# The in-projection's units in another order: those with the rotary embedding alternate with those without, and the background's share follows the kind

## The chip, the cores and the metric

One Trainium2 chip, one core of it. The metric is the device time of one launch in microseconds; of several runs the median is taken. Five engines work side by side, each with its own queue in order: TensorE (PE in the profile; its weight loads are PEld), VectorE (DVE), ScalarE (ACT), GpSimd (POOL) and SyncE (SP), whose queue starts the transfers. An instruction waits at the head of its queue until what it needs is there, and everything behind it waits too.

## What the kernel computes

One block of a network over 2,048 tokens of width 1,024, with 256 context tokens, all in 32-bit floats:

```python
h  = modulate(layer_norm(x), sh1, sc1);  hc = the same of ctx
q, k, v, u, g = split(h @ w_in)          # 512 columns each; the same of hc
q, k = apply_rope(q), apply_rope(k)      # t1*cos - t2*sin, t2*cos + t1*sin: not on v, u, g
o  = head_norm(softmax(q1 k1) v - lam * softmax(q2 k2) v)   # over tokens and context
u  = centred_conv(u, 4 taps)
r, i = sigmoid(u @ w_gates + b)          # in both directions
a  = exp(-8 r softplus(-lambda));  b = sqrt(1 - a*a) * i * u
y  = (scan(a, b) forwards + scan(a, b) backwards) * gelu(g)
x  = layer_norm(alpha * x + g1 * ([o, y] @ w_out))
x  = layer_norm(alpha * x + g2 * swiglu(modulate(x)))
```

The case is about `h @ w_in` for q, k, v and g, the rotary embedding on q and k, and the recurrence (conv, gates, scans), which runs in the background beside it.

## The kernel before

Every product is made of three matmuls (`mm3`, L142 to L144): both operands are split into a high and a low part, and high·high, high·low and low·high are summed in PSUM. Tokens come in four blocks of 512 (0 to 3) and the context. The stage of this case lies between about 208 and 704 us: the in-projection of blocks 2 and 3 (the first half, `X`), then of blocks 0 and 1 (the second half, `Y`). The normed input of a half lies in SBUF, and `run_units` walks through a list of units. A unit is a kind and a column chunk: `g`, `k` or `q` with c = 0 to 3 (128 columns each), or `v` with c = 0 or 1 (256 columns in two weight tiles).

For each unit `prep_w` loads the weights, casts the high part on ACT (L173) and subtracts it for the low part on DVE (L174, 128x1024). There are two weight tiles, and the next unit's are asked for when a unit begins. The third matmul of a product (L144; for v the second, L143) is the first that reads the low part. Per block of 512 tokens a unit of kind g, k or q is 24 matmuls of 512 columns into one PSUM tile `ps_p`, of which there are four, shared with `ps_v`:

- `g`: ACT copies the tile (L197), SP stores it. The tile is free.
- `k`, `q`: ACT copies (L197), DVE shuffles the copy (L203), multiplies the PSUM tile by cos (L204, which frees it), the shuffled one by sin (L205), and adds (L206); ACT casts the high part (L209), POOL makes the low one (L210). This is the rotary embedding.
- `v`: ACT casts out of PSUM (L248), DVE subtracts (L249).

The recurrence is a generator, `chain`, over four channel blocks: conv (ACT L540, DVE L542), gates (`ps_g`, in PSUM tiles of their own; ACT L571 sigmoids, POOL L573), then the chain proper (ACT L599, L601, L606, L610, in turn with DVE L603, L612, L614, and the four scans L620 and L621 forwards, L623 and L624 backwards; L621 and L624 span 2,048 tokens), POOL L629, and the outputs (L641 to L646 for blocks 2 and 3; L663 to L669 for blocks 0 and 1, only after all g are stored). ACT needs an ACT_TABLE_LOAD where it goes from one of these functions to another. After every block of a unit (for v every 256 tokens) `between` calls `pump(n)`, which issues the next pieces of the chain until their costs, given with each `yield`, sum to n. All of it costs about 280 of these units. A scheduler then puts each engine's instructions in an order; neither list nor pump is the last word, so the order of the built program is shown below.

In the first half the units stand as g0 to g3, v0, v1, k0 to k3, q0 to q3 (q2 and q3 by block), 5.5 after each call. The second half begins with g0 to g3 alone, 5.5 each, then `g_done`, then k0 v0 q0 k1 q1 k2 v1 q2 k3 q3 with 5 a call; call 14 (`over_lru`) issues what is left of the chain, and the ten calls after it two score steps of the attention each (`early`, up to 24).

Of the kernel before, what the change touches and what calls it, by code (L numbers as in the profile page):

```python
# [60 lines left out]
def kernel(ctx: ExitStack, tc: tile.TileContext, x, cx, prm_d, wa1, wa2, b_ada, w_in, w_v, lqk,  # L61
# [7 lines left out]
    def dma(o, i):  # L69
        return nc.sync.dma_start(out=as32(o), in_=as32(i)).ins  # L70
# [82 lines left out]
    with ExitStack() as s12:  # L153
# [61 lines left out]
        def proj_v(p, bl, ws, between, ahead):  # L215

            vw = [w.rearrange("p a k d -> p a (k d)").rearrange("p a (k d) -> p a k d", d=256) for w in ws]
            for b in bl:
                t0, W = blocks[b]
                ht = hts[b]  # L220
                pss = [psum("proj", "ps_v") for _ in range(W // 256)]

                def mms(n, t, half):
                    o = pss[n][:, t * 256:(t + 1) * 256]
                    for k in range(4):
                        h = ht[:, :, 4 * half + k, (2 * n + t) * P:(2 * n + t + 1) * P]
                        w = vw[half][:, :, k]

                        mm3(o, h[:, 0], h[:, 1], w[:, 0], w[:, 1], half == k == t == 0, half == t == 1 and k == 3)

                if b != bl[-1]:
                    for n in range(W // 256):
                        for half in range(2):
                            for t in range(2):
                                mms(n, t, half)
                else:
                    for half in range(2):
                        for n in range(W // 256):
                            for t in range(2):
                                mms(n, t, half)  # L240
                        if half == 0:
                            ahead()
                for n, ps in enumerate(pss):
                    hi = rp.tile([P, 512], F32R, tag="hi", name="vh", bufs=2)
                    lo = rp.tile([P, 512], F32R, tag="lo", name="vl", bufs=2)
                    hm = lambda a: a.rearrange("p (h t d) -> p h t d", h=2, t=2)
                    tm = ps.rearrange("p (t h d) -> p h t d", h=2, t=2)
                    last["act"] = S.copy(hm(hi), tm).ins  # L248
                    last["dve"] = V.tensor_tensor(hm(lo), tm, hm(hi.bitcast(F32)), ALU.subtract).ins  # L249
                    kt = t0 // P + 2 * n  # L250
                    for part, t in ((0, hi), (1, lo)):
                        dma(v_d[p][part, :, :, kt:kt + 2, :], hm(t))
                    between()

        base = {"q": 0, "k": 4, "g": 12}

        def run_units(units, between=lambda: None):

            ws, order_ = {}, []
            for k, c, _ in units:  # L260
                for key in ([(k, c, 0), (k, c, 1)] if k == "v" else [(k, c)]):
                    if key not in order_:
                        order_.append(key)

            def want(i):
                if i < len(order_) and order_[i] not in ws:
                    k, c, *half = order_[i]
                    ws[order_[i]] = prep_w(w_v[c, half[0]] if half else w_in[base[k] + c])

            want(0)  # L270
            for k, c, bl in units:
                if k == "v":
                    i = order_.index((k, c, 0))
                    want(i + 1)
                    proj_v(c, bl, [ws[k, c, 0], ws[k, c, 1]], between, lambda: want(i + 2))
                    continue
                want(order_.index((k, c)) + 1)
                for b in bl:
                    proj(k, c, b, ws[k, c])
                    between()  # L280

        with ExitStack() as s1:
            xp = s1.enter_context(tc.tile_pool(name="xp", bufs=8, reuse_waits="tile"))
# [188 lines left out]
            def ada_pump(n):  # L472
                for _ in range(n):
                    next(ada, None)
# [4 lines left out]
            for n, b in enumerate(order[1:], 1):  # L479
                if n + 1 < len(order):  # L480
                    load_x(order[n + 1])
                hts[b] = new_ht()
                lift(b, xt, range(KD))
                if n + 1 < len(order):
                    xt = norm(order[n + 1])
                for c in range(4):
                    ps = psum("proj", "ps_u")
                    mm_u(b, c, ps, range(KD))
                    put_u(b, c, ps)
                    ada_pump(0 if n == 1 else 2)  # L490
                if b == "c":
                    run_units([("k", c, [b]) for c in range(4)] + [("v", p, [b]) for p in range(2)], lambda: ada_pump(2))
            ada_pump(100)


# [209 lines left out]
        state = {"hold": False, "g_done": False, "end": False, "due": 0.0}  # L705
# [3 lines left out]
        def pump(n):  # L709

            state["due"] += n
            paces.append((last["act"], last["dve"]))
            act, dve = paces[max(0, len(paces) - 1 - 1)]
            while state["due"] > 0:
                if state["end"] or (state["hold"] and not state["g_done"]):
                    state["due"] = 0
                    return
                try:
                    with tc.issue_after(act), tc.issue_after(dve):
                        cost = next(bg)  # L720
                    if cost == "drained":
                        state["hold"] = True
                    else:
                        state["due"] -= cost or 1.0
                except StopIteration:
                    state["end"] = True
# [37 lines left out]

        fold = fold_wo()

        def between_x():
            next(fold, None)
            pump(5.5)

        X, Y = [2, 3], [0, 1]

        with tc.issue_after(last["x"]):
            for b in X:
                load_tabs(b)
        xs = [(k, c) for k in "gvkq" for c in range(2 if k == "v" else 4)]
        run_units([(k, c, X) for k, c in xs[:-2]] + [(k, c, [b]) for b in X for k, c in xs[-2:]], between_x)
        sf.close()
        for b in Y:
            load_ht(b)  # L780
            load_tabs(b)
        run_units([("g", c, Y) for c in range(4)], lambda: pump(5.5))
        state["g_done"] = True

        slots = {}

# [91 lines left out]
        first = s_slots(0, 0)  # L878
        calls = [0]

        def between():
            calls[0] += 1
            if calls[0] < 14:
                pump(5)
            elif calls[0] == 14:
                over_lru()
            else:
                for _ in range(2):
                    early()
# [5 lines left out]
                left[0] -= 1  # L895
                next(first)

        run_units([(k, c if k != "v" else c // 2, Y) for c in range(4) for k in ("kvq" if c % 2 == 0 else "kq")], between)

# [243 lines left out]
    units = [Unit(tb, j) for tb in range(2) for j in range(NJ)]  # L1145
# [25 lines left out]
    with ExitStack() as s4:  # L1171
# [128 lines left out]
        for b in range(NB):  # L1300
            rh = head_norm(b)
            xs = []
# [102 lines left out]
    for n in range(32):  # L1405
        hf, i = n // 16, n % 16
        c = slice(hf * 512, (hf + 1) * 512)
# [106 lines left out]
```

## Time and profile before

| | |
|---|---|
| median of 3 runs | 2916.2 us (2916.05 to 2921.6) |
| the profiled execution | 2915.73 us, span 2913.9 us |
| PE busy over the span | 2765.6 us, 95% |
| DVE busy | 2013.6 us, 69% |
| ACT busy | 1433.6 us, 49% |
| PE, DVE and ACT busy from 387 to 456 us | 51.91, 68.35 and 38.20 of 69 us |
| PE, DVE and ACT busy from 456 to 531 us | 70.14, 51.19 and 60.29 of 75 us |

The first lines are averages over a program that PE bounds nearly everywhere. The last two show that DVE's load is uneven within this stage: full where k and q run beside scans, two thirds where only g runs. What a stage loses is read from PE's waits in it and from the distance of its matmuls. The profile's busy time of PE overlaps from matmul to matmul, so the own time of a stretch is taken below as its matmuls times their distance.

### The profile page before, as it was taken

The page shows a single profiled execution, that of the slowest core. Times are in us where ns is not written, and L with a number is a line of the kernel's source. Part 1 is how long each engine was busy: PE and PEld are TensorE (multiplying, and loading weights), DVE is VectorE, ACT ScalarE, POOL GpSimd, SP SyncE. Part 2 cuts the span into 40 slices and gives each one's busy share as a digit, 9 for nine tenths or more (in the row PEclk, how much of TensorE's full clock was granted, in tenths as well). Part 3 has the DMA queues.
Part 4 walks back from the last instruction along what each step waited for, and adds up shares of the span by engine and source line. Part 5 has one row for each costly group of instructions (what it writes and reads, how often), then busy time and mean ns, then how long its engine had stood idle before and what let it go on. Part 6 is the DMA issues. An engine that isn't in the chain of part 4 may idle for free.

```text
span 2913.9 us, 37631 instructions
## 1 busy us (share of the span) xinstructions
PE 2765.6 (95%) x13452; PEld 2310.3 (79%) x13452; DVE 2013.6 (69%) x3298; ACT 1433.6 (49%) x2039; POOL 1409.1 (48%) x923
## 2 busy tenths in 40 slices
PE   8989879878999999999999899999999999999998
PEld 4868767766899999987777688887888888888886
DVE  7755796586899999995788865558656556335554
ACT  3546668663677777774235533334333334224332
POOL 2004544444788888871354754445544432112443
PEclk9999999989999999999999999999999999999999
DMA  8875637357132222217373433223322237446552
GB/s 328 315 224 177 201 107 274 119 180 224 42 76 76 72 74 61 66 41 278 128 248 101 147 96 87 81 86 115 100 85 80 80 100 258 136 130 188 164 164 90
DMA packets 227804, 407.96 MB, mean 140 GB/s; under 512 B 21400, under 2 KB 110616, under 8 KB 225056
## 3 DMA queue, kind: packets, MB, share of 16 engines
q1 hardware_dynamic: 227616, 405.55, 43.3%
q8 instruction: 106, 1.74, 0.3%
q14 instruction: 82, 0.67, 0.1%
HBM read 281.74 MB, written 123.75 MB: 139 GB/s over the span
## 4 chain that ended last, share of the span: by engine, by line
PE 66%; DVE 7%; ACT 3%; issue 2%; POOL 2%; DMA 2%; SPq 0%; DVEq 0%; ACTq 0%; POOLq 0%
PE ps L143 14%; PE ps L144 14%; PE ps L142 14%; PE ps_s L846 8%; PE pt L927 4%; PE po L921 2%; PE po L922 2%; PE po L920 2%; DVE e L848 1%; PE ps_w L1225 1%; PE ps_w L1226 1%; PE ps_w L1229 1%; PE ps_l L1225 1%; PE ps_l L1229 1%; PE ps_l L1226 1%
## 5 line engine op out<-in xcount | busy, mean ns | idle before, releaser
L848 DVE TENSOR_SCALAR_CACHE_REDUCE e<-ps_s 128x768 f32<-128x768 f32 x384 | 359.6, 951 | 37.0 <-PE ps_s L846 28.5
L864 POOL TENSOR_TENSOR a<-e,e 128x768 f32<-128x768 f32 x192 | 349.3, 1849 | 17.1 <-PE pt L927 12.5
L846 PE MATMUL ps_s<-k,q 128*128 128x384 f32 x1536 | 335.7, 350 | 13.8 <-DVE e L848 12.5
L853 ACT ACTIVATE e<-e,nm 128x2304 f32<-128x2304 f32 x128 | 285.2, 2228 | 50.6 <-DVE nm L852 47.5
L846 PEld LDWEIGHTS ps_s<-k,q 128*128 128x128 f32 x1536 | 267.2, 191 | 29.4 <-DVE e L848 22.4
L1376 ACT CAST hid<-hf 128x512 fp32r<-128x512 f32 x192 | 111.5, 586 | 281.2 <-PE ps L144 266.5
L1377 POOL TENSOR_TENSOR hid<-hf,hid 128x512 fp32r<-128x512 f32 x64 | 83.6, 1306 | 315.9 <-ACT hid L1376 315.9
L931 ACT CAST ah<-pt 128x512 fp32r<-128x512 f32 x288 | 166.1, 582 | 130.1 <-PE pt L927 128.9
L932 DVE TENSOR_TENSOR al<-pt,ah 128x512 fp32r<-128x512 f32 x288 | 196.0, 686 | 34.7 <-ACT ah L931 34.5
L1377 DVE TENSOR_TENSOR hid<-hf,hid 128x512 fp32r<-128x512 f32 (+1 forms) x128 | 95.8, 751 | 157.1 <-ACT hid L1376 157.0
L861 POOL TENSOR_SCALAR e<-e,rr,rn 128x2304 f32<-128x2304 f32 x64 | 146.4, 2288 | 90.3 <-DVE nm L852 49.9
L1053 POOL TENSOR_TENSOR s<-w1r 128x512 f32<-128x512 f32 x44 | 59.3, 1348 | 270.3 <-DMA w1r<-in_w 254.2
L142 PE MATMUL ps_p<-ht,w 128*128 128x512 f32 (+1 forms) x416 | 162.0, 390 | 18.2 <-DVE kf L204 11.6
L927 PEld LDWEIGHTS pt<-ident,a 128*128 128x128 f32 x1152 | 144.2, 141 | 42.8 <-POOL a L864 4.3
L927 PE MATMUL pt<-ident,a 128*128 128x128 f32 x1152 | 174.6, 274 | 3.6 <-POOL a L864 3.4
L144 PE MATMUL ps_p<-ht,w 128*128 128x512 f32 (+1 forms) x416 | 161.2, 389 | 7.6 <-DVE w L174 7.6
L143 PE MATMUL ps_p<-ht,w 128*128 128x512 f32 (+1 forms) x416 | 161.3, 388 | 0.0
L210 POOL TENSOR_TENSOR lo<-kf,hi 128x512 fp32r<-128x512 f32 (+1 forms) x36 | 58.7, 1633 | 177.9 <-ACT hi L209 147.1
L1097 POOL TENSOR_TENSOR v<-v,q 128x512 f32<-128x512 f32 x44 | 72.1, 1639 | 145.1 <-DVE u L1096 145.1
L920 PE MATMUL po<-ah,v 128*128 128x512 f32 x288 | 126.1, 438 | 0.6 <-ACT ah L931 0.6
L921 PE MATMUL po<-al,v 128*128 128x512 f32 x288 | 116.3, 404 | 3.8 <-DVE al L932 2.1
L922 PE MATMUL po<-ah,v 128*128 128x512 f32 x288 | 114.1, 396 | 0.0
(3086 smaller groups left out, 8298.5 us busy)
## 6 DMA issues: line engine op xcount, KB each, us to landing
w1r<-in_w SPq DMA_DIRECT2D x88, 512.0 KB, 3.5
hf<-hid_d SPq DMA_DIRECT2D x64, 512.0 KB, 4.1
hid_d<-hid SPq DMA_DIRECT2D x88, 256.0 KB, 2.2
wraw<-in_w_in SPq DMA_DIRECT2D x32, 512.0 KB, 5.1
adaw<-in_wa SPq DMA_DIRECT2D x32, 512.0 KB, 4.9
q<-q_d SPq DMA_DIRECT2D x64, 256.0 KB, 4.9
oy<-oy_d SPq DMA_DIRECT2D x16, 1024.0 KB, 5.8
x<-in_x SPq DMA_DIRECT2D x29, 512.0 KB, 8.7
```

The lines of the kernel that those rows point to most:

```text
L142: PE.matmul(ps, lhsT=lh, rhs=rh, start=start, stop=False)
L143: PE.matmul(ps, lhsT=lh, rhs=rl, start=False, stop=False)
L144: last["pe"] = PE.matmul(ps, lhsT=ll, rhs=rh, start=False, stop=stop).ins
L846: PE.matmul(ps[:, j, :384], lhsT=q[:, m, part, qt * P:(qt + 1) * P], rhs=kst[h, m][:, c0:c0 + 384], start=(part == 0), stop=(part == 1))
L848: V.tensor_scalar(et[:, cc * 768:(cc + 1) * 768].rearrange("p (a b) -> p a b", a=2), ps[:, :, :384], -0.125, None, ALU.mult, ALU.min, accu ...
L853: S.activation(et, et, AF.Exp, bias=nm[:, m:m + 1], scale=-1.0, accum_out=ss[m])
L864: last["a"] = G.tensor_tensor(a, es[0][:, g * 768:(g + 1) * 768], es[1][:, g * 768:(g + 1) * 768], ALU.add).ins
L920: PE.matmul(po, lhsT=vh, rhs=ah, start=(j == 0), stop=False)
L921: PE.matmul(po, lhsT=vh, rhs=al, start=False, stop=False)
L927: PE.transpose(pt[:, qt * P:(qt + 1) * P], ath[h, b, qt, j // 6][:, (j % 6) * P:(j % 6 + 1) * P], ident)
L932: V.tensor_tensor(al, pt, ah.bitcast(F32), ALU.subtract)
L1377: (G if m in (1, 4) else V).tensor_tensor(t[:, 1], raw[:, 4 * r:4 * r + w], t[:, 0].bitcast(F32), ALU.subtract)
```

## The change

Units now alternate in one list for each half. First half: g0 k0 g1 k1 v0 q0 g2 k2 v1 k3 g3 q1, then q2 and q3 by block. Second half: g0 k0 g1 q0 g2 k1 g3 v0 q1 k2 v1 q2 k3 q3, in one call of `run_units`. `between` gets the kind: 6.8 units of the background after a g or v, 4.2 after a k or q (in the first half 16 calls of each, 176 as before). In the second half `over_lru` comes at call 20, `g_done` after the eighth g block, and the twelve calls after call 20 make two score steps each.

```diff
-        def run_units(units, between=lambda: None):
+        def run_units(units, between=lambda kind: None):
...
-                    proj_v(c, bl, [ws[k, c, 0], ws[k, c, 1]], between, lambda: want(i + 2))
+                    proj_v(c, bl, [ws[k, c, 0], ws[k, c, 1]], lambda: between("v"), lambda: want(i + 2))
...
-                    between()
+                    between(k)
...
+        share = {"g": 6.8, "v": 6.8, "k": 4.2, "q": 4.2}
+        def between_x(kind):
             next(fold, None)
-            pump(5.5)
+            pump(share[kind])
...
-        xs = [(k, c) for k in "gvkq" for c in range(2 if k == "v" else 4)]
+        xs = [("g", 0), ("k", 0), ("g", 1), ("k", 1), ("v", 0), ("q", 0), ("g", 2), ("k", 2), ("v", 1), ("k", 3),
+              ("g", 3), ("q", 1), ("q", 2), ("q", 3)]
...
-        run_units([("g", c, Y) for c in range(4)], lambda: pump(5.5))
-        state["g_done"] = True
+        g_units = [0]
...
-        def between():
+        def between(kind):
             calls[0] += 1
-            if calls[0] < 14:
-                pump(5)
-            elif calls[0] == 14:
+            g_units[0] += kind == "g"
+            state["g_done"] = g_units[0] == 8
+            if calls[0] < 20:
+                pump(share[kind])
+            elif calls[0] == 20:
                 over_lru()
...
-        run_units([(k, c if k != "v" else c // 2, Y) for c in range(4) for k in ("kvq" if c % 2 == 0 else "kq")], between)
+        ys = [("g", 0), ("k", 0), ("g", 1), ("q", 0), ("g", 2), ("k", 1), ("g", 3), ("v", 0), ("q", 1), ("k", 2),
+              ("v", 1), ("q", 2), ("k", 3), ("q", 3)]
+        run_units([(k, c, Y) for k, c in ys], between)
```

What this does to the engines' order is shown at three places. First DVE late in the first half, around the long scans of the second channel block (gate_3081 and gate_3083 before). Before, in the middle of the k and q units:

```order
L174 TENSOR_TENSOR w<-wraw,w 128x1024
L614 SCALAR_TENSOR_TENSOR gate_3083<-A_3311,gate_3083 128x1152
L206 TENSOR_TENSOR kf<-kf,sh 128x512
L620 SCALAR_TENSOR_TENSOR gate_3081<-A_3310,gate_3081 128x256
L204 TENSOR_TENSOR kf<-ps_p,ct 128x512
L205 TENSOR_TENSOR sh<-sh,st__1988 128x512
L623 SCALAR_TENSOR_TENSOR gate_3083<-A_3311,gate_3083 128x256
L203 STREAM_SHUFFLE sh<-kf 128x512
L621 SCALAR_TENSOR_TENSOR gate_3081<-A_3310,gate_3081 128x2048
L206 TENSOR_TENSOR kf<-kf,sh 128x512
L624 SCALAR_TENSOR_TENSOR gate_3083<-A_3311,gate_3083 128x2048
L174 TENSOR_TENSOR w<-wraw,w 128x1024
```

And after, where these scans are gate_2969 and gate_2971, from the weights of q1 to behind the long scans:

```order
L174 TENSOR_TENSOR w<-wraw,w 128x1024
L614 SCALAR_TENSOR_TENSOR gate_2971<-A_3225,gate_2971 128x1152 x2
L204 TENSOR_TENSOR kf<-ps_p,ct 128x512
L205 TENSOR_TENSOR sh<-sh,st__1992 128x512
L620 SCALAR_TENSOR_TENSOR gate_2969<-A_3224,gate_2969 128x256
L206 TENSOR_TENSOR kf<-kf,sh 128x512 x2
L623 SCALAR_TENSOR_TENSOR gate_2971<-A_3225,gate_2971 128x256
L621 SCALAR_TENSOR_TENSOR gate_2969<-A_3224,gate_2969 128x2048
L174 TENSOR_TENSOR w<-wraw,w 128x1024
L624 SCALAR_TENSOR_TENSOR gate_2971<-A_3225,gate_2971 128x2048
L203 STREAM_SHUFFLE sh<-kf 128x512
L204 TENSOR_TENSOR kf<-ps_p,ct 128x512
```

Before, the L204 of k3's and q0's blocks stand ahead of, between and behind the scans, and a unit's weights (L174) behind both long ones. After, k3's rotary ends ahead of them, the next unit is g3, which has none, and the weights stand between the two long scans.

Second, DVE at the border of the halves, from the weights of the third unit of the second half (g2 before, g1 after; the first L174 of each piece) to those of the fourth. Before:

```order
L174 TENSOR_TENSOR w<-wraw,w 128x1024
L612 TENSOR_TENSOR gate_3758<-gate_3758,gate_3757 128x1152
L614 SCALAR_TENSOR_TENSOR gate_3758<-A_4010,gate_3758 128x1152
L542 SCALAR_TENSOR_TENSOR uc<-ub,prm,uc 128x2048 x2
L174 TENSOR_TENSOR w<-wraw,w 128x1024
```

After:

```order
L174 TENSOR_TENSOR w<-wraw,w 128x1024
L203 STREAM_SHUFFLE sh<-kf 128x512
L204 TENSOR_TENSOR kf<-ps_p,ct 128x512
L205 TENSOR_TENSOR sh<-sh,st__4112 128x512
L206 TENSOR_TENSOR kf<-kf,sh 128x512
L620 SCALAR_TENSOR_TENSOR gate_3715<-A_4010,gate_3715 128x256
L542 SCALAR_TENSOR_TENSOR uc<-ub,prm,uc 128x2048
L621 SCALAR_TENSOR_TENSOR gate_3715<-A_4010,gate_3715 128x2048
L542 SCALAR_TENSOR_TENSOR uc<-ub,prm,uc 128x2048
L542 SCALAR_TENSOR_TENSOR uc<-ub,prm,uc 128x256
L203 STREAM_SHUFFLE sh<-kf 128x512
L174 TENSOR_TENSOR w<-wraw,w 128x1024
```

Between the two weights stood four instructions of the chain and the conv; now k0's first rotary block and the shuffle of its second, two scans, one of them long, and three of the conv stand there.

Third, ACT late in the second half: the pieces end with the cast of q1's weights (L173), behind the last sigmoid (L571) of the last channel block; the names are that block's gates (gate_44..) and decays (A_). Before:

```order
L599 ACT_TABLE_LOAD
L599 ACTIVATE A_4758<-gate_4401,spm_1976 128x1152
L606 ACTIVATE A_4758<-A_4758,ones 128x1152
L601 ACTIVATE gate_4401<-gate_4401,spm_1975 128x1152
L571 ACT_TABLE_LOAD
L571 ACTIVATE gate_4403<-ps_g,prm 128x256
L599 ACT_TABLE_LOAD
L599 ACTIVATE A_4759<-gate_4403,spm_1976 128x1152
L197 COPY kf<-ps_p 128x512
L173 CAST w<-wraw 128x1024
```

After:

```order
L571 ACT_TABLE_LOAD
L571 ACTIVATE gate_4438<-ps_g,prm 128x256
L606 ACTIVATE A_4669<-A_4669,ones 128x1152
L601 ACTIVATE gate_4436<-gate_4436,spm_1975 128x1152
L641 ACT_TABLE_LOAD
L641 ACTIVATE gg<-gg 128x512
L599 ACT_TABLE_LOAD
L599 ACTIVATE A_4670<-gate_4438,spm_1976 128x1152
L606 ACTIVATE A_4670<-A_4670,ones 128x1152
L173 CAST w<-wraw 128x1024
```

Between the last sigmoid and the cast stood a table load and two others; now two table loads and five others stand there. The table loads of the whole program go from 59 to 63.

## Rows read from the trace of the kernel before

**Rows 1.** Windows: us, busy PE, PEld, DVE, ACT, POOL (xinstructions), PEclk, DMA, GB/s.

```profile
387.00:456.00 69.00, 51.91 (x218) 41.22 (x216) 68.35 (x76) 38.20 (x49) 30.67 (x18) 0.93 0.43 149
456.00:531.00 75.00, 70.14 (x327) 57.76 (x325) 51.19 (x42) 60.29 (x73) 27.99 (x23) 1.00 0.59 224
531.00:670.00 139.00, 117.34 (x630) 101.76 (x631) 89.69 (x85) 87.71 (x106) 64.01 (x38) 0.90 0.50 171
```

**Rows 2.** Waits of PE, 387 to 456 us: total us, times, longest.

```profile
PE ps_p L142 <- DVE kf L204: 11.6, 2, 9.3
PE ps_p L144 <- DVE w L174: 3.3, 2, 2.2
PE ps_p L142 <- ACT hi L209: 2.1, 1, 2.1
```

**Rows 3.** Timeline of PE around that longest wait: start, us, instruction [idle before].

```profile
433.59 0.77 PE L142 MATMUL ps_p<-ht,w 128*128 128x512 f32 x1 [9.34 <-DVE kf L204]
...
435.00 0.63 PE L142 MATMUL ps_p<-ht,w 128*128 128x512 f32 x1
435.43 0.63 PE L143 MATMUL ps_p<-ht,w 128*128 128x512 f32 x1
...
437.37 0.39 PE L142 MATMUL ps_p<-ht,w 128*128 128x512 f32 x1
437.60 0.40 PE L143 MATMUL ps_p<-ht,w 128*128 128x512 f32 x1
```

**Rows 4.** Waits of PE, 270 to 341 us.

```profile
PE ps_v L142 <- ACT w L173: 6.0, 1, 6.0
PE ps_v L143 <- DVE w L174: 1.5, 1, 1.5
```

**Rows 5.** Timeline of ACT: copies of the first, the last X and the last block.

```profile
219.49 0.57 ACT L197 COPY kf<-ps_p 128x512 f32<-128x512 f32 x1
...
455.36 0.58 ACT L197 COPY kf<-ps_p 128x512 f32<-128x512 f32 x1
...
703.96 0.59 ACT L197 COPY kf<-ps_p 128x512 f32<-128x512 f32 x1
```

**Rows 6.** Groups by shape, 208 to 705 us: busy us, mean ns, idle before.

```profile
L174 DVE TENSOR_TENSOR w<-wraw,w 128x1024 fp32r<-128x1024 f32 x30 | 47.4, 1582 | 31.1 <-ACT w L173 31.0
...
L206 DVE TENSOR_TENSOR kf<-kf,sh 128x512 f32<-128x512 f32 x31 | 35.3, 1137 | 0.3
...
L542 DVE SCALAR_TENSOR_TENSOR uc<-ub,prm,uc 128x2048 f32<-128x2048 f32 x12 | 30.0, 2503 | 14.6 <-ACT uc L540 14.6
...
L203 DVE STREAM_SHUFFLE sh<-kf 128x512 f32<-128x512 f32 x32 | 23.7, 741 | 0.0
...
L612 DVE TENSOR_TENSOR gate<-gate,gate 128x1152 f32<-128x1152 f32 x16 | 22.7, 1423 | 11.2 <-ACT gate L610 11.0
...
L204 DVE TENSOR_TENSOR kf<-ps_p,ct 128x512 f32<-128x512 f32 x31 | 21.2, 684 | 1.0
...
L621 DVE TENSOR_TENSOR_SCAN gate<-A,gate 128x2048 f32<-128x2048 f32 x4 | 19.0, 4739 | 0.0
```

**Rows 7.** Waits of PE, 456 to 531 us.

```profile
PE ps_p L142 <- DMA ht<-ht_d: 1.0, 1, 1.0
```

**Rows 8.** Waits of PE, 531 to 670 us.

```profile
PE ps_v L142 <- DVE kf L204: 5.5, 2, 4.3
PE ps_v L143 <- DVE w L174: 4.6, 3, 3.9
PE ps_v L142 <- ACT w L173: 4.5, 2, 4.0
```

**Rows 9.** Timeline of ACT around a table load in the second half.

```profile
558.86 0.58 ACT L248 CAST vh<-ps_v 128x512 fp32r<-128x512 f32 x1
559.46 1.28 ACT L599 ACT_TABLE_LOAD   x1
560.75 1.26 ACT L599 ACTIVATE A<-gate,spm 128x1152 f32<-128x1152 f32 x1
```

More of the change, by code (lines that the diff above doesn't have):

```diff
@@ L491 @@
                 if b == "c":
-                    run_units([("k", c, [b]) for c in range(4)] + [("v", p, [b]) for p in range(2)], lambda: ada_pump(2))
+                    run_units([("k", c, [b]) for c in range(4)] + [("v", p, [b]) for p in range(2)], lambda _: ada_pump(2))
             ada_pump(100)
@@ L765 @@
         fold = fold_wo()
-        def between_x():
+        share = {"g": 6.8, "v": 6.8, "k": 4.2, "q": 4.2}
+        def between_x(kind):
             next(fold, None)
-            pump(5.5)
+            pump(share[kind])
         X, Y = [2, 3], [0, 1]
```

## The prediction, made before the changed kernel had run

> **What bounds the kernel now.** I read the windows first, because the page's averages hide the stage. From 387 to 456 us DVE is busy 68.35 of 69 us while PE is busy 51.91; from 456 to 531 it is the reverse, PE 70.14 and DVE 51.19 of 75 [rows 1]. So the first half of the in-projection ends on DVE, with k's and q's rotary beside the chain's scans, and the border of the halves, with g alone, ends on PE. The waits of PE name it: 11.6 us for the L204 that frees a PSUM tile, 3.3 for weights, 2.1 for L209, 17.0 in all [rows 2]. The longest, 9.34, is followed by matmuls 0.43 us apart, where later ones are 0.23 apart [rows 3]: the granted clock had fallen to its lower level. Ahead of that stretch PE waits 7.5 us for the weights of v [rows 4]. From 531 to 670 three kinds of wait sum to 14.6 [rows 8].
>
> PE's own work in a half is its matmuls by their distance, 0.227 us for 512 columns (the 0.23 of [rows 3], less rounded) and, as an estimate from that, half of it, 0.115, for 256. A half has 24 unit-blocks of 24 matmuls (130.8 us) and 384 narrow ones of v (44.2). With the background's gates, one channel block is 48 wide and 12 narrow ones, 12.3 us. The first half, from the copy of the first block to that of the last, 219.49 to 455.36, is 235.9 us [rows 5] for 130.8 - 5.4 + 44.2 + 24.6 = 194.2 of matmuls: 41.6 lost. The second, to 703.96, is 248.6 for about 205: 44 lost. The sum below is made against the profiled execution's 2915.7 us; the median is 2916.2, half a us more. I call same what is within 0.2%, 5.8 us, which is about what a measurement of this kernel can tell from no change.
>
> **What is changed in amount.** Matmuls, rotary blocks, chain and weights are the same in number. Four table loads more at 1.28 us [rows 9] are 5.1 us of ACT, and count only where ACT is waited for (below). The background's total share in the first half is unchanged, so what moves is which DVE and ACT work falls beside which matmuls. Four score steps more are asked for early, twelve calls of two instead of ten, but by the order of PE as many stand ahead of the last q in both: nothing, since work that came earlier there would only change its place.
>
> **First half, its end.** Between the weights of g3 and those of q3, DVE has in the new order three L174 (1.58), seven of L603, L612 and L614 (1.42 by L612), four each of L203 (0.74), L204 (0.68) and L205 (about 1), three L206 (1.14), two long scans (4.74) and two short ones (about 1, an estimate from L204 and L206): 4.7 + 10.0 + 3.0 + 2.7 + 4.0 + 3.4 + 9.5 + 2.0 = 39.3 us [rows 6]. PE has 130 matmuls there, 29.5 us. PE therefore loses about 9.8, if DVE is in step with it at the start, in four or five pieces of one to three us, too short for a pause like that of [rows 3]. Before, the 69 us of [rows 1] held 218 matmuls, 49.5 us: 19.5 lost. Gain 9.7. It can be nothing (DVE late at g3 by as much) and at most the whole 19.5.
>
> **First half, v.** v's second weights cannot be cast before the unit ahead has left its weight tile. Before, some 5 us of v's matmuls stood ahead of their first use, and PE waited 6.0 + 1.5 [rows 4]. After, the first channel block's gates stand among v0's matmuls, 10 us by the order, and this wait goes. What is late next is a PSUM tile: v0's last L249 stands behind a long scan and eight more instructions of the chain, and I make PE 6 us late there, at g2, and 1 us at a sigmoid. Of 7.5 plus a stretch at the lower clock, 7 remain: gain 3, between -3 and 7.5.
>
> **The border.** PE waited 1.0 us at most there [rows 7]. After, between the weights of g1 and of q0, DVE has one rotary block (3.5 us), the next one's L203 (0.74), two scans (1 and 4.74), two long conv steps (2.50), a short one (0.6, an estimate by its 256 columns from the 512 of L204), and L174 (1.58): 17.2 us [rows 6] beside 48 matmuls, 10.9. That is a wait of 6.3, or 4.7 with uncontended durations. In front of it, counted the same way, ACT has 14.8 us from the channel block's last gates to the cast of g1's weights, two table loads among them, beside 11.4 of matmuls: 3.4 late. Before, nothing was to be had there: 327 matmuls at 0.227 are 74 of the 75 us [rows 1]. The two together are 10 at most; with the lower price of the one, 3.4 of the other and what the two waits share (DVE is early at q0 by what PE lost at g1), I take +6, between 0 and +10.
>
> **The end.** v0 followed k0 and waited for its weights (most of the 4.6 and 4.5 of [rows 8], 9.1); now it follows g3, and the gates stand among its matmuls again; 2 remain: -7. q1's weights are cast on ACT behind the last channel block. From the last 512-column sigmoid to that cast I count 7 table loads (9.0 us) and 14 others (12.2: six of 1,152 columns at 1.26 and the rest at about 0.58, both as in [rows 9]) against 4 loads and 12 others (15.5) before; PE has 11.3 us of matmuls there and so waits 9.9 instead of about 2: +8. The scans of the last block with k's and q's rotary follow in both, and by the order they cost the same. Sum +1, between -7 and +10.
>
> The Trainium skill, ScalarE: Activation LUTs, section "What ACT_TABLE_LOAD costs", speaks against this part: it gives a switch to another function's set 1.28 us for the load and 1.38 for a drain, 2.66 in all. The trace does not show the drain: a cast ends at 559.44, the load runs from 559.46 to 560.74, and the next ACTIVATE starts at 560.75 [rows 9]. With the drain, the 7 loads ahead of q1's weights would cost 9.7 more.
>
> **Sum.** -9.7 - 3 + 6 + 1 = -5.7: 2915.7 - 5.7 = 2910.0, at the edge of what can be told from no change.
>
> **Rivals.** *The second half takes more than the first gives (slower).* One mechanism: the chain of the last two channel blocks has to go through ACT and DVE in queue order, and in the new order rotary blocks and outputs stand in that queue ahead of weights that PE needs at once. Price: the border at its +10, and q1's wait +8 with no credit for v0, +18; with a gain of only 6 in the first half (DVE late at g3), 2928. It decides from where the second half loses some 12 us more than its 44. For it speaks that DVE has 51.19 of 75 us at the border [rows 1] and gets four rotary blocks more, 14 us, and that the two pieces are in-order facts. Against: DVE has 24 us free there.
> *No change.* DVE has the same work in the stage, and the chain the same length; the waits could move within the stage and sum to the same. For it: the first half's gain and the second's loss have opposite signs and similar sizes; 2916.
> *More than forecast.* All 17.0 + 7.5 us of the first half's waits go [rows 2, 4] and the second loses nothing: 2891.
> *Table loads that cost more.* If ACT stands still for 1.38 us more after each load, the loads ahead of q1's weights bring the second half up by 9.7 and the whole to 2919.7, which is no change. By the trace the next instruction starts at once [rows 9], so 0.02. This is the drain of the Trainium skill's page named above.
> *The change does not do what it says* (the scheduler undoes it): the order shows that it does not; no chance of weight.
>
> **How the numbers follow.** Forecast (2901 to 2914) 0.38, more than forecast 0.10, no change 0.26 (waits moved 0.24, table loads 0.02), slower 0.26. The forecast's own interval has some 0.34 of its 0.38 below 2910.4, 5.8 us under the median, and 0.04 above, so faster by over 0.2% 0.44, within 0.30, slower 0.26. The range for 8 in 10 goes down to 2891, where all waits of the first half are gone, and up to 2931, the slower case with 3 us more for the lower clock: by [rows 3] eight matmuls after a long wait cost 0.2 us each, 1.6, and two such pauses are possible.
>
> **What would show it.** Right: between the copies of the first and the last block of the first half about 223 us instead of 235.9, no wait for L204 near 9 us there; in the second half about 256, with new waits of PE for L174 at q0 and for L173 at q1 of 5 to 10 us each. The forecast is wrong if the first half is not shorter by 8 us, or if the second is longer by more than 12. If q1's wait is near 20, ACT is slower around table loads than [rows 9] shows.

## The result and the profile after

The changed kernel takes 2934.9 us (median of 4 runs, 2929.8 to 2936.7); the kernel before, on the same chip, 2916.9. The ratio is 1.0059, 95% interval 1.0044 to 1.0074: slower by 17 us. The forecast was 2910.0, the range ended at 2931. The profiled execution took 2935.13 us, its span is 2933.3.

Most of it arises in the in-projection: the last block's copy begins 18.0 us later than in [rows 5], of the 19.4 us between the two spans. What follows is nearly even, but only in sum: from the last matmul of the in-projection to the last of the attention (`po`) 652.4 us where it was 655.4, and from there to the end 1559.5 where it was 1555.0. The copies of the first, the last X and the last block:

```profile
217.92 0.59 ACT L197 COPY kf<-ps_p 128x512 f32<-128x512 f32 x1 [4.10 <-PE ps_p L144]
...
464.70 0.61 ACT L197 COPY kf<-ps_p 128x512 f32<-128x512 f32 x1
...
721.98 0.59 ACT L197 COPY kf<-ps_p 128x512 f32<-128x512 f32 x1 [3.46 <-PE ps_p L144]
```

The middle one stands behind sigmoids on ACT; PE had ended the first half at 458.6 (before: 451.5). So I measure on PE: from the first to the last in-projection matmul of a half, less its matmuls by their distance (0.227 and 0.115 us, as in the prediction). By that the first half loses 44.0 us (before 40.8), the second 60.8 (before 47.3). The halves themselves take 246.5 us (before 240.6) and 262.9 (before 252.1): 12 gate matmuls of the third channel block, 2.7 us, have moved from the second half into the first. The windows that answer to [rows 1] (us; busy PE, PEld, DVE, ACT, POOL; PEclk; DMA; GB/s):

```profile
387.00:456.00 69.00, 62.91 (x262) 50.73 (x261) 59.56 (x61) 40.86 (x50) 25.56 (x16) 0.93 0.42 143
456.00:531.00 75.00, 67.15 (x275) 52.91 (x274) 49.43 (x48) 59.41 (x71) 26.26 (x19) 0.93 0.58 216
531.00:670.00 139.00, 108.99 (x592) 95.16 (x591) 88.44 (x75) 89.59 (x103) 61.67 (x37) 0.91 0.42 145
```

The first is better by 11 us of PE, the other two worse, and the border's clock is 0.93 where it was 1.00. (The windows are fixed in time, and the halves' border has moved from 451.5 to 458.6.) PE's waits (total us, times, longest), first from 387 to 456 us, to be set beside [rows 2]:

```profile
PE ps_p L144 <- DVE w L174: 6.1, 2, 3.2
```

Then from 270 to 387, beside [rows 4]:

```profile
PE ps_v L142 <- ACT w L173: 5.1, 1, 5.1
PE ps_p L144 <- DVE w L174: 4.1, 1, 4.1
PE ps_p L142 <- DVE vl L249: 3.8, 1, 3.8
PE ps_v L143 <- DVE w L174: 3.6, 1, 3.6
PE ps_g L142 <- ACT gate L571: 3.4, 2, 2.2
```

From 456 to 531, where [rows 7] had 1.0:

```profile
PE ps_p L144 <- DVE w L174: 2.7, 2, 1.4
PE ps_g L142 <- ACT gate L571: 2.4, 2, 2.3
PE ps_p L142 <- ACT w L173: 2.2, 1, 2.2
PE ps_p L142 <- DMA ht<-ht_d: 0.4, 1, 0.4
```

And from 531 to 690, beside [rows 8]:

```profile
PE ps_v L142 <- DVE kf L204: 12.2, 3, 7.1
PE ps_p L142 <- ACT w L173: 8.8, 1, 8.8
PE ps_g L142 <- ACT gate L571: 4.9, 2, 2.7
PE ps_g L142 <- ACT gh L552: 3.7, 1, 3.7
PE ps_v L143 <- DVE w L174: 1.9, 1, 1.9
...
```

The 8.8 is q1's weights. On ACT they stand behind the last channel block, with a table load ahead of nearly every function (start, us, instruction):

```profile
603.62 1.28 ACT L571 ACT_TABLE_LOAD   x1
604.91 0.47 ACT L571 ACTIVATE gate<-ps_g,prm 128x256 f32<-128x256 f32 x1
605.28 1.24 ACT L606 ACTIVATE A<-A,ones 128x1152 f32<-128x1152 f32 x1
606.43 1.24 ACT L601 ACTIVATE gate<-gate,spm 128x1152 f32<-128x1152 f32 x1
607.69 1.28 ACT L641 ACT_TABLE_LOAD   x1
608.98 0.63 ACT L641 ACTIVATE gg<-gg 128x512 f32<-128x512 f32 x1
609.63 1.28 ACT L599 ACT_TABLE_LOAD   x1
610.92 1.25 ACT L599 ACTIVATE A<-gate,spm 128x1152 f32<-128x1152 f32 x1
612.09 1.24 ACT L606 ACTIVATE A<-A,ones 128x1152 f32<-128x1152 f32 x1
613.23 1.03 ACT L173 CAST w<-wraw 128x1024 fp32r<-128x1024 f32 x1
```

A load is 1.28 us as in [rows 9], and what follows starts at once. ACT is busy 70.85 of the 75 us around it (after, then before; columns as above):

```profile
560.00:635.00 75.00, 60.37 (x340) 53.19 (x341) 28.66 (x27) 70.85 (x78) 20.66 (x16) 0.91 0.34 112
```

```profile
560.00:635.00 75.00, 60.13 (x253) 48.31 (x253) 52.89 (x52) 58.33 (x64) 22.02 (x13) 0.89 0.38 132
```

### The profile page after: what moved, and what is told of

Same layout as the page of the kernel before. It is cut to its first block, busy times and chain, and to the rows that moved or that the text cites. A ratio compares the mean times of both kernels' runs of the same rounds, so it can differ in the third digit from the quotient of the medians.

```text
span 2933.3 us, 37617 instructions
## 1 busy us (share of the span) xinstructions
PE 2773.1 (95%) x13452; PEld 2314.8 (79%) x13452; DVE 2013.5 (69%) x3298; ACT 1439.6 (49%) x2043; POOL 1417.8 (48%) x923
## 4 chain that ended last, share of the span: by engine, by line
PE 63%; DVE 7%; issue 3%; POOL 2%; DMA 2%; ACT 1%; SPq 1%; DVEq 0%; ACTq 0%; POOLq 0%
PE ps L143 14%; PE ps L144 14%; PE ps L142 14%; PE ps_s L849 8%; PE pt L934 4%; PE po L928 2%; PE po L929 2%; PE po L927 2%; DVE e L851 1%; SPq L70 1%; DMA w1r<-in_w 1%; PE ps_l L1232 1%; PE ps_l L1233 1%; PE ps_l L1236 1%; PE ps_w L1232 1%
## 5 line engine op out<-in xcount | busy, mean ns | idle before, releaser
L142 PE MATMUL ps_p<-ht,w 128*128 128x512 f32 (+1 forms) x416 | 164.8, 396 | 17.3 <-ACT w L173 11.0
L934 PEld LDWEIGHTS pt<-ident,a 128*128 128x128 f32 x1152 | 144.3, 141 | 41.1 <-POOL a L867 2.6
L144 PE MATMUL ps_p<-ht,w 128*128 128x512 f32 (+1 forms) x416 | 162.4, 394 | 12.9 <-DVE w L174 12.9
L143 PE MATMUL ps_p<-ht,w 128*128 128x512 f32 (+1 forms) x416 | 163.2, 392 | 0.0
```

Of the source, the lines that this page charges most:

```text
L142: PE.matmul(ps, lhsT=lh, rhs=rh, start=start, stop=False)
L143: PE.matmul(ps, lhsT=lh, rhs=rl, start=False, stop=False)
L144: last["pe"] = PE.matmul(ps, lhsT=ll, rhs=rh, start=False, stop=stop).ins
L934: PE.transpose(pt[:, qt * P:(qt + 1) * P], ath[h, b, qt, j // 6][:, (j % 6) * P:(j % 6 + 1) * P], ident)
```

## The experiments

Times are compared by the ratio to the kernel before, measured beside each kernel on the same chip, and in us of 2916.5. "Lost" is PE's loss in the two halves as defined above, from one profile each; profiles with the same first half differ by up to 5 us in it.

**Which half, or the share?** e1 is the kernel before with the first half's list and share; e2 has the second half's list, share and limits; e3 is the changed kernel with even shares; e4 is the kernel before with the shares alone:

```diff
e1 (on before)  - xs = [(k, c) for k in "gvkq" ...]; pump(5.5)   + xs, share as changed
e2 (on changed) - xs as changed; pump(share[kind]) in X          + xs as before; pump(5.5) in X
e3 (on changed) - pump(share[kind])                              + pump(5.5) in X, pump(5.8) in Y
e4 (on before)  - pump(5.5), pump(5)                             + pump(share[kind])
```

> The first half's new order with its kind-dependent share, the second half's order and share as before. Theory A (the loss is made in the second half: its border and its end, +13 us of waits and 7 us of lower clock; in the first half the end's gain of 11 us and v's loss of 9 cancel): +1 to +3 us against the kernel before, 2918 to 2920, and PE's waits for v's second weights (L174, then L173, 3 to 5 us each) are in the trace. Rival B (the first half's v is what costs: its waits push everything behind it later): +8 us or more. Rival C (the unequal shares cost, not the orders): +6 to +9.

> The first half as before, the second half's new order with its kind-dependent share and its 20th-call limit. Theory A (the loss is made in the second half): +13 to +17 us, 2930 to 2934, with waits of PE for q0's weights (L174) and q1's (L173, about 9 us) as in the changed kernel. Rival B (the first half's v is what costs): +8 us or less. Rival C (the unequal shares): +6 to +9.

> Both halves in the new order, the share equal for all kinds of unit: 5.5 in the first half (the same sum, 176), 5.8 in the second (110.2 instead of 111.0 up to the 20th call). Theory A (the orders cost, by weights that stand behind the background's work in the queues of DVE and ACT): within 5 us of the changed kernel, 2930 to 2940; the waits move to other units, their sum stays. Rival C (the unequal shares are the cause): back to 2917 or less.

> Both halves in the order of before, with the kind-dependent share (6.8 for g and v, 4.2 for k and q) alone. Theory A: within 5 us of the kernel before, 2912 to 2922, of either sign, because the shares only shift which unit gets which of the background's instructions. Rival C (the unequal shares are the cause): +10 us or more, 2927 and up.

| run | us | ratio (95%) | lost, first + second | last long scan begins |
|---|---|---|---|---|
| before | 2916.9 | 1 | 40.8 + 47.3 | 621.7 |
| changed | 2934.9 | 1.0059 (1.0044 to 1.0074) | 44.0 + 60.8 | 644.5 |
| e1 | 2917.0 | 1.0005 (0.9996 to 1.0014) | 42.6 + 48.4 | 625.0 |
| e2 | 2909.5 | 0.9975 (0.9967 to 0.9984) | 39.9 + 44.4 | 625.3 |
| e3 | 2944.4 | 1.0097 (1.0084 to 1.0111) | 37.0 + 73.3 | 676.3 |
| e4 | 2932.8 | 1.0055 (1.0042 to 1.0067) | 38.1 + 55.4 | 657.4 |

All three theories fall: one half alone does nothing, the other alone gains 7 us, and both together lose 17; e4 comes out as C has it, e3 the other way. e3 and e4 lose least in the first half and more in the second, where the chain's last long scan (L624) comes late. Not all of this is the chain: in e3, 12.5 us of PE's waits at the border are for the normed input (DMA `ht`; in the changed kernel 0.4), 6.6 of them between the halves and counted in the 73.3; and in e4 PE ends the stage when the kernel before does (703.6 us, before 703.5). What e4 loses shows behind it: the 32 score matmuls that stood in the stage begin only at 708.5 (before: at 679.5), and PE waits 4.6 us for `k` there. The second half of e2 and that of the changed kernel are the same code, but the scheduler put their instructions in different orders.

**The order, or what the first half leaves?** In the kernels that follow every engine's order is held by edges that order two instructions without a wait, at the end of the kernel function (shortened; names stand for the numbers of the program's instructions):

```diff
+    for names in issue_order.values():      # per engine: the order wanted
+        for a, b in zip(names, names[1:]):
+            tc.add_manual_dep(made[b], a, NoSync)
```

p1 is the changed kernel with e2's order from the border to the end, p2 is e2 with the changed kernel's, p7 is e1 with that of the kernel before.

> The changed kernel with its own first half; from the border of the halves to the end every engine's instructions are held in the order that they have in the kernel with the second half's change alone (2909.5 us). Nothing else differs. Theory D (the two halves' changes, -0.4 and -8 us alone and +18 together, differ through the order that the scheduler makes of the second half, which is another one behind the new first half): 2905 to 2915. Rival E (the same order would cost the same 18 us, because the new first half leaves chain, clock or queues behind it in another state): 2930 or more.

> The kernel with the second half's change alone (first half as before), and from the border of the halves to the end every engine's instructions in the order of the changed kernel. Theory D (the order made of the second half is the cause): 2928 to 2938, with the waits of PE for q1's weights (8.8 us) and for k2's L204 (7.1 and 4.0). Rival E (the state that the new first half leaves): 2906 to 2914.

> The kernel with the first half's change alone, and from the border of the halves to the end every engine's instructions in the order of the kernel before: the third order of the second half beside the two of the runs with held orders, in both of which the new first half cost 7.5 to 8 us. Theory K (the new first half is worth nothing in itself, and leaves the recurrence's chain 3 to 4 us further back against PE at the border, which the second half pays): 2922 to 2927. Rival L (the new first half costs nothing, as its run with a second half that the scheduler ordered anew, 2917.0, suggests; the 7.5 to 8 us belong to the two other orders): 2915 to 2919.

| from the border on, order of | old first half | new first half | difference |
|---|---|---|---|
| before | 1 | p7: 1.0015 (1.0006 to 1.0024) | +4.4 us |
| e2 | e2: 0.9975 | p1: 0.9998 (0.9989 to 1.0007) | +6.7 |
| changed | p2: 1.0038 (1.0024 to 1.0052) | 1.0059 | +6.1 |

p1 (2917.0 us) and p2 (2927.0) lie between the ranges of D and E, nearer to D: each is a part. From the border to the end the changed kernel's order costs 18 us more than e2's (columns: 0.0063 and 0.0061) and 11 us more than before's; the new first half costs 4 to 7 us behind each held order. The 4.4 is the least sure: e1 has p7's order in both halves but for one short conv step, and another only behind them, and is 3 us better; their intervals overlap.

The held order runs to the end of the program, and the 18 us are not all of this stage. From the attention's last matmul (`po`) to the end, the four profiles in e2's order (e2, p1, r3, s1; the last two are described below) take 1551.8 to 1553.4 us, the seven in the changed order (changed, p2, p3, p4, q3, r2, r4) 1558.9 to 1561.9, before and p7 1555.0 and 1554.4. So some 8 of the 18 us are lost behind the attention; what loses them there stays open. The second half itself takes 12.6 us more in p2 than in e2, and 10.9 more in the changed kernel than in p1.

What the new first half costs is smaller in place: it loses 2.3 us more (mean of seven profiles 43.4, of five with the old one 41.1). For the rest K says that it hands the chain over further back. One milestone agrees: the third channel block's last sigmoid begins 34.0 us behind PE's end of the first half with the new one (changed, p1, p7) and 30.9 to 31.2 with the old (before, e2, p2). But that block's last long scan does not keep the lag: it begins 78.2 us behind this end in the changed kernel and 77.0 in p2, 78.3 in p1 and 77.9 in e2, 68.6 in p7 and 68.8 before. So K's time just came in (2922.0), its mechanism is not shown, and where the rest of the 4 to 7 us goes stays open.

**Are PE's waits what is lost?** p3 and p4 hold the changed kernel's order and move only what PE waited for:

```diff
p3  DVE + L174 (v0's second weights)   ACT + L173 (v1's second weights)
          L542 x3                            L759 (waits for POOL)
        - L174                             - L173
    also L174 of q0 ahead of L612, L614; L249 ahead of L621
p4  ACT: L173 of q1 ahead of the block's last L571; DVE: both L204 of k2 behind their L203
```

> The changed kernel with the order of every engine held as it is, but for four instructions of the first half that stand further ahead in their queue: on DVE v0's second weights (L174) ahead of two long conv steps, q0's weights (L174) ahead of L612 and L614, v0's third L249 ahead of the long scan L621; on ACT v1's second weights (L173) ahead of the cast L759 that waits for POOL. Theory F (a wait of PE that is taken away is won, and with it the stretch at the lower clock behind it): waits of 3.6, 3.1, 3.8 and 4.1 us are 14.6, half of the stretches at half clock behind them (3.4, 3.4, 3.4, 6.8) 8.5: 2912 to 2921. Rival G (DVE and ACT bound this stage, so the wait turns up at the next unit): 2930 or more.

> The changed kernel with the order of every engine held as it is, but for three instructions of the second half: on ACT q1's weights (L173) ahead of the last channel block's last sigmoid, exponential and output with their table loads, on DVE the two L204 of k2 right behind their shuffles, ahead of L665, L643 and L206. Theory F (a wait that is taken away is won, with the lower clock behind it): waits of 8.4, 5.6 and 4.0 us are 18.0, half of the stretches at half clock behind them (10.2, 6.8, 3.4) 10.2: 2907 to 2917. Rival G (DVE and ACT bound this stage, the wait turns up at the next unit): 2930 or more.

Measured: p3 2935.8 (1.0068, 1.0055 to 1.0080), p4 2933.2 (1.0058, 1.0045 to 1.0070): nothing won, rival G. In p3 the 16.6 us at the four places (v1's weights are 5.1 in the trace, where the expectation has 3.1) became others. From 270 to 387 us the waits sum to 19.8 us; without the four moves they were 20.0:

```profile
PE ps_p L142 <- DVE vl L249: 6.1, 3, 2.8
PE ps_g L142 <- ACT gate L571: 3.6, 3, 2.2
PE ps_g L142 <- ACT gh L552: 3.5, 1, 3.5
PE ps_v L142 <- DVE kf L204: 2.0, 1, 2.0
PE ps_p L142 <- ACT w L173: 1.4, 1, 1.4
PE ps_p L144 <- DVE w L174: 1.2, 2, 0.8
PE ps_v L143 <- DVE w L174: 1.1, 1, 1.1
PE ps_v L142 <- ACT w L173: 0.9, 1, 0.9
```

The chain does not come sooner: the second block's first sigmoid begins at 361.9, in the changed kernel at 362.1. In p4 q1's cast began at 598.9 instead of 613.2, but its L174 only at 605.4, behind an L603 that waits for ACT, and PE waited for this and for v1's (531 to 690 us):

```profile
PE ps_v L143 <- DVE w L174: 9.1, 2, 7.2
PE ps_p L144 <- DVE w L174: 5.4, 2, 4.5
...
```

Of the second half's waits 4.6 us less remain in p4 than in the changed kernel, of some 18 that were taken away. The last long scan begins at 645.1 in p3 and at 640.0 in p4 (changed: 644.5). e2 shows as well that such a wait is a poor measure: it waits longer for q1's weights than the changed kernel and is 25 us faster (531 to 690 us):

```profile
PE ps_p L142 <- ACT w L173: 9.5, 1, 9.5
...
```

**Is it ACT's function switches?** q3 (changed) and q4 (before) hold all orders and put tanh in place of root and gelu, so that the loads between the functions go; their values are others. r2 groups ACT's functions in the last block of the changed kernel, r3 in e2. r4 and s1 move only a few:

```diff
q3, q4: - AF.Sqrt, AF.Gelu_apprx_tanh   + AF.Tanh        (63 -> 38, 59 -> 36 loads)
r2, r3: 40 instructions of ACT: all sigmoids, exp/tanh, roots, gelus  (63 -> 48, 57 -> 47)
r4: L641 x2 to the gelu L663; last L571 ahead of L610, L599          (63 -> 58)
s1: the same on e2, sigmoids together                                (57 -> 52)
```

> The changed kernel with all orders held and the chain's root and gelu replaced by tanh, so that its values are others: 63 table loads become 38, 25 x 1.28 = 32 us less of ACT over the two halves, every instruction but the loads in its place. Theory H (the table loads lengthen the chain that the stage waits for): 2910 to 2922. Rival G: 2930 or more.

> The kernel before, all orders held, with the chain's root and gelu replaced by tanh, so that its values are others: 59 table loads become 36, 23 x 1.28 = 29 us less of ACT. Theory M (both kernels wait for the chain through ACT, the changed one only longer, because its order switches more often where ACT is full): the gain is smaller than the changed kernel's 21.6 us, 2905 to 2912, and the two kernels without switches (2913 for the changed one) lie within 8 us. Rival N (the switches cost both kernels the same, and the 18 us between them have another cause): 2893 to 2899.

> The changed kernel with the order of every engine held, but for 40 instructions of ACT in the second half (from the last channel block's first exponential to the casts of k2's and v1's weights): its sigmoids first, then exponentials and tanh, then the roots, then the gelus. The program's table loads go from 63 to 48, 15 x 1.28 = 19 us of ACT, where ACT is busy without a pause from 575 to 627 us. Theory H (the chain of the last channel block, through ACT, is what the second half waits for): the last long scan (L624, at 644.5) begins 10 us or more earlier and the time is 2917 to 2927. Rival G (what is taken from one wait turns up at the next, DVE behind it): 2931 or more.

> The same grouping of ACT's 40 instructions in the kernel with the second half's change alone (2909.5), all other orders held: 57 table loads become 47, 10 x 1.28 = 12.8 us of ACT. Theory H (the chain through ACT is what the second half waits for): the last long scan earlier than 625 by 5 us or more, 2898 to 2905. Rival G: 2907 to 2914.

> The changed kernel, all orders held but for ACT's in the last channel block: two gelus (L641) of the outputs moved to the gelu behind them, the block's last sigmoid ahead of a root and an exponential; nothing of the chain is put later than it was but these two outputs, which DVE reads 50 us on. 63 table loads become 58, 5 x 1.28 = 6.4 us in ACT's full stretch from 575 to 627 us. Theory M: the last long scan 5 to 8 us earlier than 644.5, PE's wait for q1's weights (8.8) shorter by about 6, the time 2922 to 2930. Rival N: 2932 or more.

> The kernel with the second half's change alone (2909.5), all orders held but for ACT's in the last channel block: the last sigmoids stand together, ahead of two roots, and two gelus of the outputs stand with the gelus behind the chain; 57 table loads become 52, 6.4 us of ACT. No gelu is needed sooner by DVE, and the first exponentials stay where they are (in the grouped version of the same kernel, 2913.0, they had to wait for all sigmoids). Theory M (each switch less in ACT's full stretch is won): 2900 to 2906. Rival N (this kernel's stage no longer waits for ACT): 2907 to 2913.

| run | us | ratio (95%) | lost | last long scan |
|---|---|---|---|---|
| q3 | 2913.3 | 0.9991 (0.9982 to 1.0000) | 38.8 + 43.4 | 619.9 |
| q4 | 2902.5 | 0.9948 (0.9936 to 0.9960) | 36.6 + 35.4 | 606.9 |
| r2 | 2931.7 | 1.0050 (1.0036 to 1.0064) | 46.6 + 52.1 | 638.2 |
| r3 | 2913.0 | 0.9988 (0.9979 to 0.9996) | 40.4 + 48.3 | 634.0 |
| r4 | 2926.9 | 1.0030 (1.0018 to 1.0042) | 42.8 + 49.2 | 631.2 |
| s1 | 2908.2 | 0.9969 (0.9959 to 0.9980) | 41.2 + 43.2 | 627.3 |

Without these switches the changed kernel gains 20 us by the ratios (theory H), the one before 15, so both wait for ACT, the changed one somewhat more; q4 fell between theories M and N, and 12 us remain between q3 and q4 (4 of them behind the attention). r4, with five loads fewer and nothing left out, gains 8 us (theory M); from the loads' own 6.4 this cannot be told, and r4 also moves two gelus and a sigmoid. Its ACT has 63.43 us of work where the changed kernel's has 70.85, and its waits from 531 to 690 us show where the gain is; what stays is DVE's:

```profile
560.00:635.00 75.00, 65.12 (x373) 57.41 (x372) 40.43 (x34) 63.43 (x73) 19.92 (x15) 0.93 0.42 141
```

```profile
PE ps_v L142 <- DVE kf L204: 12.7, 3, 6.2
...
PE ps_p L142 <- ACT w L173: 0.6, 1, 0.6
...
```

r2 saved 15 loads and r3 ten, and neither is told from the kernel it was made from (3 us less and 4 us more, the intervals overlap; both times are G's). In both the chain's first exponential waits for all sigmoids (590.1 in r2, 577.1 in the changed kernel), which may be why; it was not tested by itself, and r2's last long scan still begins 6 us sooner. s1 is not told from e2 either (rival N): in e2's order ACT works 57.37 of those 75 us, and five loads fewer win nothing that shows. e2 and s1 are better than both kernels.

## Why the prediction was wrong

It was wrong in sign: -5.7 forecast, +17 measured. The main step that failed is "First half, v": its waits were forecast to fall and rose, so the first half, forecast 12.7 us better, loses 3.2 more. By the prediction's own sign that alone refutes it: between the copies of the half's first and last block stand 246.8 us, where it wanted about 223 instead of 235.9. The second is "The end": +1 forecast, +8 measured. In terms of PE's loss the steps read as follows.

- *First half, its end*, -9.7: right in mechanism, too large. The waits from 387 to 456 us went from 17.0 [rows 2] to 6.1, and the 9.3 for L204 is gone. But from 387 us to the half's end PE loses 12.4 us where it lost 17.5, 5.1 less. The step's "too short for a pause like that of [rows 3]" did not hold: each of the two waits left, 2.9 and 3.2 us, is followed by about eight matmuls 0.43 us apart, at the lower of the clock's two levels (0.51 granted from 428.7 to 432.0 us):

```profile
427.67 0.50 PE L144 MATMUL ps_p<-ht,w 128*128 128x512 f32 x1 [2.92 <-DVE w L174]
...
429.25 0.63 PE L143 MATMUL ps_p<-ht,w 128*128 128x512 f32 x1
429.67 0.63 PE L144 MATMUL ps_p<-ht,w 128*128 128x512 f32 x1
```

- *First half, v*, -3: failed; ahead of 387 us PE loses 31.7 us where it lost 23.4, +8.3. Of v's second weights the step says "this wait goes"; v0's are still waited for (3.6), and v1's (5.1) had no term: its L173 stands on ACT behind L759, which waits for POOL. q0's weights (4.1) had none either. The two that were foreseen came smaller and larger: the bank at g2 3.8 instead of 6, the sigmoids 3.4 instead of 1. Ahead of 387 there are 20.0 us of waits where there were 12.6: 7.5 in [rows 4], 0.9 at sigmoids, and before 270 and behind 341 us

```profile
PE ps_g L142 <- ACT gh L552: 2.1, 1, 2.1
PE ps_g L142 <- ACT uh L581: 2.1, 1, 2.1
```

The step added up waits as independent terms. p3 shows that they are not: where it moves what four of them waited for, the sum of the waits stays the same.
- *The first half's price behind it*, not in the sum: it loses 3.2 us more in place (2.3 in the mean of the profiles), and costs 4 to 7 in all.
- *The border*, +6: right. Waits went from 1.0 [rows 7] (1.5 with a shorter one) to 7.7 us, made up otherwise than forecast: the g1 cast 2.2 (3.4 forecast), L174 2.7 in two (6.3 forecast for one), sigmoids 2.4 (no term). With the lower clock (0.93 in the window above, 1.00 in [rows 1]), PE loses 14.1 us in the first 79 of the second half, where it lost 8.9: +5.2.
- *The end*, +1: failed; in the rest of the second half PE loses 46.6 us where it lost 38.4. The two terms that it had came near: q1's weights 8.8 (9.9 forecast), and v's waits for weights 9.1 to 1.9 (forecast to 2). The second is luck in part: of the 9.1, put down to v0, only 4.3 stood in its matmuls (523.5 to 564 us) and 4.8 in v1's (from 626.9), and the 1.9 that is left is v1's. What failed is "the scans of the last block ... cost the same": k2's L204 stood behind L624 and two L665, 12.2 us in all for L204 where [rows 8] had 5.5. The gates' waits (L571, L552), 8.6 us where they were 4.9, had no term. The two parts of the second half, +7 in the forecast, are +13.5 in place and +9 behind the old first half (p2, 56.3).
- *Table loads*: the rival that gave each a further 1.38 us is refuted by the rows above. But "count only where ACT is waited for" was the wrong place to stop: in the last channel block ACT is waited for, and r4, with five of them fewer, is 8 us faster.
- *The slower rival* (2928) had the mechanism of the second half, in-order queues with the chain's last blocks ahead of weights, and its price of some 12 us more than the 44; it still credited the first half with 6. It is the rival that came nearest.

What stays open: what holds the chain in the new first half (its second block's first sigmoid comes 35.7 us behind the end of the first block's last scan L624, before 28.4), how the new first half costs more than it loses in place, what the changed order loses behind the attention, and most of the 12 us between the two kernels without switches.

## What to carry to other kernels

Where a serial background runs through the same in-order queues as the foreground, do not add up the foreground's waits as if each could be won alone: in p3 and p4 the waits that were taken away came back at other units. Look at the background's own milestones beside them. The start of the last long scan is one: among the kernels in the changed order the fastest has it first (q3, 619.9 us) and the slowest last (p3, 645.1). It does not rank kernels of different orders (e1 and e2 both have it at 625 us, and their times are 7.5 us apart), so it is a guide and not a price. And where a scheduler orders the program, hold one part's order while changing another before crediting a change with an effect, and look to the program's end for what the order does: the same second half, with what follows it, was worth -7 or +11 us by its order alone.

## What was not expected of the hardware

Short waits went with a lower clock: the border's longest wait is 2.3 us, and its granted clock is 0.93, where with one wait of 1.0 and one of 0.5 it was 1.00 [rows 1, 7]. Behind q1's wait PE runs at half rate, 0.43 us a matmul:

```profile
614.31 0.79 PE L142 MATMUL ps_p<-ht,w 128*128 128x512 f32 x1 [8.76 <-ACT w L173]
614.90 0.63 PE L143 MATMUL ps_p<-ht,w 128*128 128x512 f32 x1
615.33 0.63 PE L142 MATMUL ps_p<-ht,w 128*128 128x512 f32 x1
```

One and the same DVE instruction, the 128x1024 L174, took 1.21 us while POOL was idle and 3.39 while it worked; the L174s of [rows 6] averaged 1.58, so a sum made with that mean is short where POOL runs the outputs (L669) and long where it is idle. DVE, then POOL (idle from 598.9 to 632.0 us) in the changed kernel:

```profile
625.45 1.21 DVE L174 TENSOR_TENSOR w<-wraw,w 128x1024 fp32r<-128x1024 f32 x1
...
657.95 3.39 DVE L174 TENSOR_TENSOR w<-wraw,w 128x1024 fp32r<-128x1024 f32 x1
```

```profile
650.11 7.36 POOL L629 TENSOR_TENSOR gate<-gate,gate 128x512 f32<-128x512 f32 x4 [4.36 <-DVE gate L624]
657.43 2.82 POOL L669 TENSOR_TENSOR gg<-gg,hs 128x1024 fp32r<-128x1024 f32 x1
```

The Trainium skill, SBUF — State Buffer, section "SBUF: two separate sides", says that a DVE instruction with two SBUF inputs and one of GpSimd that reads SBUF lock each other out for a whole instruction. The rows agree: L174 begins at 657.95, while L669 runs to 660.25, and ends at 661.34, 1.1 us behind it, about the 1.21 that it takes alone. No run here took POOL's work away to show it.
